# The meta tokens' share of an attention product, taken over 128 rows instead of 16, and one transpose moved to another PSUM buffer

## The chip, the cores and the metric

The kernel runs on one core of a Trainium2 chip. Its engines are TensorE (PE; its weight loads are shown apart as PEld), VectorE (DVE), ScalarE (ACT), GpSimd (POOL) and SyncE (SP), each with its own instruction queue and in step only through semaphores. The metric is the device time of one execution in microseconds (us); the lower the better. The median of three runs of the kernel before is 1240.04 us (1238.72 to 1245.06).

## The reference

One layer of a hybrid decoder, for one prompt of 512 tokens behind 16 learned meta tokens, and for 8 sequences that decode one token each over 2048 cached positions. RMSNorm, one input projection (2048 to 8192 columns), then eight heads of a gated linear recurrence and eight heads of differential attention, one output projection with the residual, final RMSNorm. All in float32. The part around the change is the attention of the prompt:

```python
def diff_attend(q, k, v, q_pos, k_pos, rel_bias, lam):
    s = jnp.einsum('bqhcd,bkhcd->bchqk', qf, kf) * (AT_DQK ** -0.5)
    dist = q_pos[:, None] - k_pos[None, :]
    bias = jnp.transpose(rel_bias[rel_bucket(dist)].astype(jnp.float32), (2, 0, 1))
    s = jnp.where(dist >= 0, s + bias, NEG_INF)
    p = jax.nn.softmax(s, axis=-1)
    w = p[:, 0] - lam * p[:, 1]
    return jnp.einsum('bhqk,bkhv->bqhv', w, v.astype(jnp.float32))
...
k_prompt (DEPTH, BATCH, N_META+SEQ, ...)   v_prompt   k_sample   v_sample    # new rows, also outputs
```

Keys 0 to 15 are the meta tokens, keys 16 to 527 the prompt. So the weights w of a block of 128 queries are a strip of 16 meta columns and one to four blocks of 128 columns, and the output is a sum of products over those blocks, the last of them over only 16 keys.

## The kernel before

**Projections.** The weights come in 128-column blocks (64 of the input projection, 16 of the output projection). ACT splits a group of four 128x128 tiles into a rounded part `hi` and DVE makes the rest `lo`; PE multiplies them with the split activations, 24 matmuls a group into the tile `ps`, four groups a block. The order is aq, ak, av (eight blocks each), then the recurrence's blocks, the gates, the output. One group is one slot of the main loop (line 1338); `split` runs three groups ahead (`LEAD`, line 296).

**Threads.** Everything else is written as Python generators that give out a few instructions in each slot, behind the group's matmuls: `attn_head`, `attn`, `hgrn`, the softmax of the decode sequences, and so on. `fill` and `value_step` add steps of the decode attention (key pages on DVE: `pgt`, `scd`; value pages on PE: `t_pv`) when a cost model of the five engines (class `Clock`) says that there is time and that a page has landed. Tiles taken through `tp` and `sc` are known to that model as rings of two PSUM buffers. All this happens while the program is written; on the chip each engine runs its list in that order.

**Attention of a head.** `to_tok` (lines 876 to 889) transposes the head's values on PE into two PSUM tiles of the ring `tp`: 24 rows (16 meta tokens and 8 samples) and 4 x 128 prompt rows. ACT copies both into one SBUF tile `vtok` of five 128-column parts (two buffers, shared with `ktok`), and three stores send the parts to the outputs from ACT's queue. `attn` (line 931) then works in steps n, four for a head; the block j of step n is scored at n, exponentiated at n+1, combined at n+2, transposed at n+3 and multiplied with the values at n+4. For two blocks together the output is built in the one PSUM buffer `o` (pool `psv`, tag `pv`) by matmuls of 256 columns (256 and 128 for the diagonal), and a last one, line 947, adds the meta tokens from 16 rows:

```python
T.matmul(o[:, :2 * P], a["vtok"][0:NM, 4, :], a["wmT"], start=False, stop=True)
```

Each float32 matmul is two in the trace. The transposes of a block, `t_w`, go to a `tp` buffer; the transposed meta strip fits beside them for blocks 0 to 2, and takes a second `tp` buffer, `t_w2`, for the fourth block (line 961). ACT copies them to `wT` and `wmT`.

When a head's block 3 is multiplied with the values, the step also holds the transposes of the values of the next head but one. Since the values of two heads fit in `vtok`'s buffers, ACT's copies there wait for the product `o` of the older head, which stands behind the transposes on PE; the next `t_w` takes the PSUM buffer of the 24 rows.

Of the kernel before, what the change touches and what calls it, by code (L numbers as in the profile page):

```python
# [18 lines left out]
P = 128  # L19
# [3 lines left out]
NS = 8  # L23
# [186 lines left out]
def layer_kernel(ctx: ExitStack, tc: tile.TileContext, A):  # L210
# [297 lines left out]
    lb = cp.tile([P, H], F32, name="lb")  # L508
    lb1 = cp.tile([P, H], F32, name="lb1")
    bm = cp.tile([P, 3, H], F32, name="bm")  # L510
    bdec = cp.tile([P, NPG, 2 * H], F32, name="bdec")
    b_far, b_near, b_new = bm[:, 0, :], bm[:, 1, :], bm[:, 2, :]
    rowd = dr.tile([H, W], F32, name="rowd")
    skew = dr.tile([H, P * W], F32, name="skew")
# [5 lines left out]
    def small_constants():  # L520
        t = tp("t_rows")
        T.transpose(t[:, :18], rows, ident[:18, :18])
        V.tensor_copy(cols, t[:, :18])
        V.tensor_scalar(gat, cols[:, 17:18], 1.0 - LAM_INIT, None, op0=ALU.mult)
        V.tensor_tensor(dp, dlv[:, :, 0, :], dlv[:, :, 1, :], op=ALU.mult)
        dsum = sm.tile([P, 2], F32, name="dsum", bufs=1)
        V.tensor_reduce(dsum, dp, axis=AX.X, op=ALU.add)
        lbm = sm.tile([P, H], F32, name="lbm", bufs=1)
        lbe = sm.tile([P, 2, H], F32, name="lbe", bufs=1)
        lbr = cols[:, 0:16].rearrange("p (r h) -> p r h", r=2)  # L530
        V.tensor_tensor(lbm, lbr[:, 0, :], lbr[:, 1, :], op=ALU.max)
        V.tensor_tensor(lbe, lbr, lbm.unsqueeze(1).to_broadcast([P, 2, H]), op=ALU.subtract)
        yield
        S.activation(dsum, dsum, AF.Exp)
        S.activation(lbe, lbe, AF.Exp)

        brow = hw.tile([H, W], F32, name="brow", tag="brow")
        for c0, c1 in ((0, 512), (512, W)):
            t = tp("t_br")
            T.matmul(t[:H, :c1 - c0], relb, oh[:, c0:c1], start=True, stop=True)  # L540
            V.tensor_scalar(brow[:, c0:c1], t[:H, :c1 - c0], -1.0, None, op0=ALU.mult)
        yield
        V.tensor_tensor(nlam, dsum[:, 1:2], dsum[:, 0:1], op=ALU.subtract)
        V.tensor_scalar(nlam, nlam, -LAM_INIT, None, op0=ALU.add)
        V.tensor_tensor(lbm, lbe[:, 0, :], lbe[:, 1, :], op=ALU.add)
        V.reciprocal(lbm, lbm)
        V.tensor_tensor(lb, lbe[:, 0, :], lbm, op=ALU.mult)
        V.tensor_scalar(lb1, lb, -1.0, 1.0, op0=ALU.mult, op1=ALU.add)
        yield
        store(out=rowd, in_=brow)  # L550
        t = tp("t_bm")
        for i in range(3):
            T.matmul(t[:, i * H:(i + 1) * H], oh[:, OF + i * P:OF + (i + 1) * P], relb, start=True, stop=True)
        V.tensor_copy(bm.rearrange("p m h -> p (m h)"), t[:, :3 * H])
        for c in range(2):
            bv = bdec.rearrange("p g (h c) -> p g h c", c=2)[:, :, :, c]
            V.tensor_copy(bv[:, 0:NPG - 1, :], b_far.unsqueeze(1).to_broadcast([P, NPG - 1, H]))
            V.tensor_copy(bv[:, NPG - 1, :], b_near)
        for h in range(H):
            yield  # L560
            store(out=skew[h].rearrange("(p w) -> p w", w=W), in_=rowd[h:h + 1, :].to_broadcast([P, W]))
        flag("const")
# [16 lines left out]
    gSa = cp.tile([P, H, NS], F32, name="gSa")  # L579
    amask = [cp.tile([P, P], F32, name=f"am{i}") for i in range(2)]  # L580
    ktail = [cp.tile([P, 2 * NM], F32, name=f"kt{i}") for i in range(2)]
    for a in amask + ktail:
        G.memset(a, 0.0)


# [211 lines left out]
    def softmax_dec(s):  # L797
        sco = scs[s]
        scp = sco[:, 0:NPG, :]
        V.tensor_tensor(scp, scp, bdec, op=ALU.add)  # L800
        V.tensor_copy(sco[:, NPG, :], snew[:, s].rearrange("p h c -> p (h c)"))
        mx = sm.tile([P, 2 * H], F32, name="mx", bufs=1)
        V.tensor_reduce(mx, sco.rearrange("p g a -> p a g"), axis=AX.X, op=ALU.max)
# [72 lines left out]
    def to_tok(src, h, name, tag, dst, dst_s):  # L876

        t2 = tp("t2_" + name)
        T.transpose(t2[:NM + NS, 0:P], src[:, NKEY:CT], ident)
        t = tp("t_" + name)  # L880
        for j in range(4):
            T.transpose(t[:, j * P:(j + 1) * P], src[:, NM + j * P:NM + (j + 1) * P], ident)
        tok = hw.tile([P, 5, P], F32, name=name, tag=tag, bufs=2)
        S.copy(tok[:NM + NS, 4, :], t2[:NM + NS, 0:P])
        S.copy(tok[:, 0:4, :].rearrange("p j d -> p (j d)"), t)
        store(out=dst[0, 0, NM:NKEY, h, :].rearrange("(j p) d -> p j d", p=P), in_=tok[:, 0:4, :])
        store(out=dst[0, 0, 0:NM, h, :], in_=tok[0:NM, 4, :])
        store(out=dst_s[0, :, 0, h, :], in_=tok[NM:NM + NS, 4, :])
        return tok

    def k_out(h):
        to_tok(ak[h], h, "ktok", "t5", A["k_prompt"], A["k_sample"])
# [20 lines left out]
    def attn_head(h):  # L913
        av = avs[h]
        strip = hw.tile([P, 528], F32, name="strip", tag="t1", bufs=2)
        flat = skew[h]
        clock.arrive(strip, 0.25)
        load(out=strip, in_=bass.AP(tensor=flat.tensor, offset=flat.offset, ap=[[W - 1, P], [1, 528]]))
        vtok = to_tok(av, h, "vtok", "t5", A["v_prompt"], A["v_sample"])
        G.tensor_copy(avS[:, :, h], av[:, T0:CT])  # L920
        for c in range(2):
            cs = slice(c * 64, (c + 1) * 64)
            G.tensor_copy(ktail[h % 2][cs, c * NM:(c + 1) * NM], ak[h][cs, SEQ:NKEY])
        heads[h] = dict(h=h, strip=strip, vtok=vtok, nm=sm.tile([P, 3, 4], F32, name="nm"),
                        s1=sm.tile([P, 4, 2], F32, name="s1"))
        flag(f"head{h}")
        yield
# [3 lines left out]
    def attn():  # L931
        live = {}
        for n in range(4 * H + 4):
            h, j = divmod(n, 4)
            if n < 4 * H and j == 0:
                if f"head{h}" not in flags or flags[f"head{h}"] >= slot[0]:
                    yield f"head{h}"
                head = heads[h]
            i4, i3, i2, i1 = (live.get(n - d) for d in (4, 3, 2, 1))
            if i4:  # L940
                a, jj = i4["head"], i4["j"]
                if jj % 2:
# [1 line left out]
                    for i in range(jj):  # L944
                        T.matmul(o[:, :2 * P], a["vtok"][:, i, :], a["wT"][:, (2 * i + 1) * P:(2 * i + 3) * P], start=i == 0, stop=False)
                    T.matmul(o[:, P:2 * P], a["vtok"][:, jj, :], a["wT"][:, 0:P], start=False, stop=False)
                    T.matmul(o[:, :2 * P], a["vtok"][0:NM, 4, :], a["wmT"], start=False, stop=True)
                    S.copy(aq[:, a["h"], (jj - 1) * P:(jj + 1) * P], o[:, :2 * P])
                if jj == 3:
                    flag(f"attn{a['h']}")  # L950
# [2 lines left out]
            if i3:  # L953
# [4 lines left out]
                for i in range(jj + 1):  # L958
                    x = NM + (i - odd) % (jj + 1) * P
                    T.transpose(t[:, i * P:(i + 1) * P], i3["p"][0][:, x:x + P], ident)  # L960
                t2, c2 = (t, L2) if jj < 3 else (tp("t_w2"), 0)
                T.transpose(t2[:NM, c2:c2 + P], i3["p"][0][:, 0:NM], ident)
                if not odd:
                    a["wT"] = hw.tile([P, 7 * P], F32, name="wT", tag="t4", bufs=1)
                    a["wmT"] = sm.tile([NM, 2 * P], F32, name="wmT", tag="wmT", bufs=1)
                w2 = a["wT"].rearrange("p (c q) -> p c q", q=P)
                S.copy(w2[:, 0:2 * jj + 1:2] if odd else w2[:, 1:2 * jj + 2:2], t[:, :L2].rearrange("p (c q) -> p c q", q=P))
                S.copy(a["wmT"][:, odd * P:(odd + 1) * P], t2[:NM, c2:c2 + P])
            if i1:
                a, L1 = i1["head"], (i1["j"] + 1) * P + NM  # L970
                for c in range(2):
# [47 lines left out]
    def hgrn(h):  # L1019
# [23 lines left out]
        vt = tp("t_hvt")  # L1043
        for j in range(4):
            T.transpose(vt[:, j * P:(j + 1) * P], v[:, NM + j * P:NM + (j + 1) * P], ident)
        hv8 = sm.tile([NS, P], F32, name="hv8", tag="wmT", bufs=1)
        S.copy(hv8, t[:NS, 0:P])
        store(out=hvd[h], in_=hv8)
        vkm = sm.tile([NM, 2, P], F32, name="vkm", bufs=1)
# [376 lines left out]
```

## Time and profile before

| | |
|---|---|
| median of three runs (lowest to highest) | 1240.04 us (1238.72 to 1245.06) |
| the profiled execution | 1245.11 us |
| its span, first to last instruction | 1243.3 us |
| PE busy / DVE / ACT / POOL | 97% / 72% / 43% / 12% |
| mean granted clock of TensorE | 0.990 of full speed |
| PE's share of the chain that ended last | 79% (`ps` alone 65%) |

The attention of the prompt lies between about 258 and 470 us of the span, with its value products from 267 us on. A row of the timeline gives start, duration, engine, line, operation, the tile written and those read, the count, and in brackets the idle time of the engine before it with what ended it. All compute instructions have line 168, the helper that records them, so the tiles' names tell them apart. A PE that the profile calls busy may still stream less than it could: the weight load before a matmul and the time between two starts show that.

### The profile page before, as it was taken

How to read it: one execution, taken by the hardware profiler on the slowest of the kernel's cores; microseconds unless marked ns; L12 is line 12 of the kernel's file. 1: busy time of each engine (PE TensorE's matmuls, PEld its weight loads, DVE VectorE, ACT ScalarE, POOL GpSimd, SP SyncE). 2: the span in 40 equal slices, each digit the busy share in tenths (PEclk: the TensorE clock that was granted, in tenths of full speed). 3: DMA queues.
4: the chain of work that ended last, by engine and by line, in shares of the span. 5: the costliest groups of instructions: out<-in, count | busy, mean ns of one | idle time of the engine just before them, and what ended most of it. 6: DMA issues, size and time to landing. Idle time of an engine off the chain costs nothing.

```text
span 1243.3 us, 24937 instructions
## 1 busy us (share of the span) xinstructions
PE 1207.9 (97%) x9352; PEld 1094.5 (88%) x9352; DVE 897.7 (72%) x1678; ACT 532.6 (43%) x1255; POOL 143.2 (12%) x151
## 2 busy tenths in 40 slices
PE   8999999999999999999999999999999999999995
PEld 6899999986677677888888889999999999999995
DVE  7522498878888888878897886989988956345253
ACT  6322333344545564445355465565422235323223
POOL 2000000100000000012010120122123310022020
PEclk9999999999999999999999999999999999999998
DMA  7353788836666669888888976757978837432223
GB/s 232 98 161 93 238 280 289 287 119 220 223 224 207 187 215 305 287 279 267 290 276 289 324 242 204 240 169 243 268 215 247 257 99 238 115 91 86 86 69 138
DMA packets 240958, 261.03 MB, mean 210 GB/s; under 512 B 8783, under 2 KB 198962, under 8 KB 240171
## 3 DMA queue, kind: packets, MB, share of 16 engines
q1 hardware_dynamic: 57298, 164.09, 38.3%
q10 hardware_dynamic: 183538, 95.34, 27.0%
q8 instruction: 74, 1.21, 0.4%
q14 instruction: 48, 0.39, 0.1%
HBM read 245.94 MB, written 16.14 MB: 211 GB/s over the span
## 4 chain that ended last, share of the span: by engine, by line
PE 79%; DVE 10%; DMA 4%; ACT 3%; issue 2%; ACTq 1%; SPq 0%; DVEq 0%
PE ps L168 65%; PE t_pv L168 4%; DVE qb L168 2%; DVE pgt L168 2%; DVE scd L168 2%; PE o L168 1%; PE ho L168 1%; DVE lo L168 1%; DMA raw<-in_w_out 1%; PE sc L168 1%; DMA raw<-in_w_in 1%; PE up L168 1%; PE t_w L168 1%; PE at L168 1%; DVE p L168 1%
## 5 line engine op out<-in xcount | busy, mean ns | idle before, releaser
L168 PE MATMUL ps<-xh,hi 128*128 128x264 f32 (+2 forms) x2048 | 539.8, 294 | 1.2 <-ACT ak L168 0.8
L168 PE MATMUL ps<-xl,hi 128*128 128x264 f32 (+2 forms) x2048 | 522.5, 286 | 1.1 <-DVE xl L168 1.1
L168 PEld LDWEIGHTS ps<-xh,hi 128*128 128x128 f32 x2048 | 387.5, 189 | 51.6 <-issue 41.7
L168 DVE TENSOR_TENSOR lo<-raw,hi 128x512 fp32r<-128x512 f32 x321 | 253.5, 795 | 216.5 <-ACT hi L168 215.6
L168 PEld LDWEIGHTS ps<-xl,hi 128*128 128x128 f32 x2048 | 388.0, 189 | 2.8 <-issue 2.7
L168 PE MATMUL ps<-xh,lo 128*128 128x264 f32 (+2 forms) x2048 | 333.1, 285 | 0.0
L168 ACT CAST hi<-raw 128x512 fp32r<-128x512 f32 x321 | 196.2, 617 | 242.9 <-PE ps L168 196.0
L168 PEld LDWEIGHTS ps<-xh,lo 128*128 128x128 f32 x2048 | 283.9, 189 | 0.0
L168 DVE TENSOR_TENSOR pgt<-pgt,qb 128x1024 f32<-128x1024 f32 x128 | 156.3, 1221 | 11.7 <-DMA pgt<-in_cache_k 7.0
L168 DVE TENSOR_REDUCE scd<-pgt 128x16 f32<-128x1024 f32 x128 | 155.6, 1216 | 1.7
L168 PE MATMUL ps<-mh,hi 128*128 128x256 f32 (+1 forms) x512 | 129.9, 286 | 0.2 <-ACT y L168 0.2
L168 PE MATMUL ps<-ml,hi 128*128 128x256 f32 (+1 forms) x512 | 128.5, 283 | 0.0
L168 DVE SCALAR_TENSOR_TENSOR qb<-pgt,wd,qb 128x128 f32<-128x128 f32 x360 | 106.8, 371 | 0.0
L168 PEld LDWEIGHTS ps<-mh,hi 128*128 128x128 f32 x512 | 96.5, 188 | 0.7 <-ACT y L168 0.4
L168 PEld LDWEIGHTS ps<-ml,hi 128*128 128x128 f32 x512 | 96.6, 189 | 0.0
L168 PE MATMUL ps<-mh,lo 128*128 128x256 f32 (+1 forms) x512 | 82.4, 283 | 0.0
L168 PEld LDWEIGHTS ps<-mh,lo 128*128 128x128 f32 x512 | 70.3, 189 | 0.0
L168 PE MATMUL t_pv<-pgt,wd 128*32 128x512 f32 x320 | 48.2, 648 | 8.5 <-ACT wmT L168 4.6
L168 POOL TENSOR_TENSOR sd<-sd,vb 128x1024 f32<-128x1024 f32 x8 | 19.4, 2430 | 174.5 <-ACT vb L168 174.5
L168 ACT COPY hgm<-ho 128x128 f32<-128x128 f32 x32 | 8.5, 265 | 70.0 <-PE ho L168 69.9
L168 ACT ACTIVATE p<-p,nm 128x144 f32<-128x144 f32 (+3 forms) x64 | 36.1, 565 | 2.0 <-DVE nm L168 2.0
L168 DVE TENSOR_TENSOR xr<-xr,t_y 128x512 f32<-128x512 f32 (+1 forms) x17 | 11.2, 657 | 31.2 <-PE t_y L168 31.2
(242 smaller groups left out, 1156.0 us busy)
## 6 DMA issues: line engine op xcount, KB each, us to landing
pgt<-in_cache_k SPq DMA_DIRECT2D x128, 512.0 KB
pgt<-in_cache_v SPq DMA_DIRECT2D x128, 512.0 KB
raw<-in_w_in ACTq DMA_DIRECT2D x125, 512.0 KB
raw<-in_w_out ACTq DMA_DIRECT2D x32, 512.0 KB
x<-in_x_prompt SPq DMA_DIRECT2D x4, 1024.0 KB
qb<-qd SPq DMA_DIRECT2D x8, 512.0 KB
sd<-in_state_hgrn SPq DMA_DIRECT2D x8, 512.0 KB
vb<-hvd SPq DMA_DIRECT2D x8, 512.0 KB
```

What stands on the lines that cost most here:

```text
L168: r = f(*a, **k)
```

## The change

1. The meta rows of the values get a tile of their own, `few` (24 x 128, one buffer), in place of the fifth part of `vtok`; `hv8` of the recurrence shares its tag. `vtok` has four parts.
2. Two constant tiles `vmeta` (128 x 128) and one `wmeta` (128 x 256) are zeroed once by POOL. Once a head ACT copies the 16 meta rows of `few` into `vmeta`; the transposed meta weights go to the first 16 rows of `wmeta` instead of `wmT`. The last matmul of `o` runs over all 128 rows, of which 112 are zeros.
3. The fourth block's `t_w2` comes from `psv`, the buffer of `o`, instead of the ring `tp`, and is no longer known to the cost model.
4. The bias of the decode scores, `bdec`, holds its two different rows instead of sixteen; adding it takes two DVE instructions instead of one.

```diff
@@ small_constants
-    bdec = cp.tile([P, NPG, 2 * H], F32, name="bdec")
+    bdec = cp.tile([P, 2, 2 * H], F32, name="bdec")
...
-            bv = bdec.rearrange("p g (h c) -> p g h c", c=2)[:, :, :, c]
-            V.tensor_copy(bv[:, 0:NPG - 1, :], b_far.unsqueeze(1).to_broadcast([P, NPG - 1, H]))
-            V.tensor_copy(bv[:, NPG - 1, :], b_near)
+            V.tensor_copy(bdec.rearrange("p g (h c) -> p g h c", c=2)[:, :, :, c], bm[:, 0:2, :])
...
-    for a in amask + ktail:
+    vmeta = [cp.tile([P, P], F32, name=f"vm{i}") for i in range(2)]
+    wmeta = cp.tile([P, 2 * P], F32, name="wmeta")
+    for a in amask + ktail + vmeta + [wmeta]:
         G.memset(a, 0.0)
@@ softmax_dec
-        V.tensor_tensor(scp, scp, bdec, op=ALU.add)
+        V.tensor_tensor(sco[:, 0:NPG - 1, :], sco[:, 0:NPG - 1, :], bdec[:, 0, :].unsqueeze(1).to_broadcast([P, NPG - 1, 2 * H]), op=ALU.add)
+        V.tensor_tensor(sco[:, NPG - 1, :], sco[:, NPG - 1, :], bdec[:, 1, :], op=ALU.add)
@@ to_tok
-        tok = hw.tile([P, 5, P], F32, name=name, tag=tag, bufs=2)
-        S.copy(tok[:NM + NS, 4, :], t2[:NM + NS, 0:P])
-        S.copy(tok[:, 0:4, :].rearrange("p j d -> p (j d)"), t)
-        store(out=dst[0, 0, NM:NKEY, h, :].rearrange("(j p) d -> p j d", p=P), in_=tok[:, 0:4, :])
-        store(out=dst[0, 0, 0:NM, h, :], in_=tok[0:NM, 4, :])
-        store(out=dst_s[0, :, 0, h, :], in_=tok[NM:NM + NS, 4, :])
-        return tok
+        tok = hw.tile([P, 4, P], F32, name=name, tag=tag, bufs=2)
+        few = sm.tile([NM + NS, P], F32, name="few", tag="few", bufs=1)
+        S.copy(few, t2[:NM + NS, 0:P])
+        S.copy(tok.rearrange("p j d -> p (j d)"), t)
+        store(out=dst[0, 0, NM:NKEY, h, :].rearrange("(j p) d -> p j d", p=P), in_=tok)
+        store(out=dst[0, 0, 0:NM, h, :], in_=few[0:NM, :])
+        store(out=dst_s[0, :, 0, h, :], in_=few[NM:NM + NS, :])
+        return tok, few
@@ attn
                 head = heads[h]
+                S.copy(vmeta[h % 2][0:NM, :], head["few"][0:NM, :])
...
-                    T.matmul(o[:, :2 * P], a["vtok"][0:NM, 4, :], a["wmT"], start=False, stop=True)
+                    T.matmul(o[:, :2 * P], vmeta[a["h"] % 2], wmeta, start=False, stop=True)
...
-                t2, c2 = (t, L2) if jj < 3 else (tp("t_w2"), 0)
+                t2, c2 = (t, L2) if jj < 3 else (psv.tile([P, 512], F32, name="t_w2", tag="pv"), 0)
...
-                    a["wmT"] = sm.tile([NM, 2 * P], F32, name="wmT", tag="wmT", bufs=1)
...
-                S.copy(a["wmT"][:, odd * P:(odd + 1) * P], t2[:NM, c2:c2 + P])
+                S.copy(wmeta[0:NM, odd * P:(odd + 1) * P], t2[:NM, c2:c2 + P])
@@ hgrn
-        hv8 = sm.tile([NS, P], F32, name="hv8", tag="wmT", bufs=1)
+        hv8 = sm.tile([NS, P], F32, name="few", tag="few", bufs=1)
```

Three places show what the change does to the instruction lists. The first is ACT's list at the step with a head's last product, before (`vtok` are the values, `aq<-o` is the copy of the product, `raw` a load of projection weights):

```order
L168 COPY vtok<-t_vtok 24x128 [waits PE_49]
L168 COPY vtok<-t_vtok 128x512
L886 DMA out_v_prompt<-vtok 128x4x128 [waits DMAHW3_49,Activation_49]
L887 DMA out_v_prompt<-vtok 16x128 [waits DMAHW4_49]
L888 DMA out_v_sample<-vtok 8x128 [waits DMAHW6_49]
L168 COPY aq<-o 128x256
L168 COPY wT<-t_w 128x128 [waits PE_49]
```

The same place now, with the first instructions of the next step:

```order
L168 COPY few<-t_vtok 24x128 [waits DMAHW3_49,DMAHW2_49,PE_49]
L168 COPY vtok<-t_vtok 128x512 [waits PE_49]
L888 DMA out_v_prompt<-vtok 128x4x128 [waits Activation_49]
L889 DMA out_v_prompt<-few 16x128 [waits DMAHW4_49]
L890 DMA out_v_sample<-few 8x128 [waits DMAHW5_49]
L168 COPY aq<-o 128x256 [waits PE_49]
L168 COPY wT<-t_w 128x128 [waits PE_49]
L168 COPY wmeta<-t_w 16x128
L168 ACTIVATE p_3602,s_3385<-p_3602,nm 128x400 [waits DVE_49]
L168 ACTIVATE p_3604,s_3385<-p_3604,nm 128x400 [waits DVE_49]
L168 CAST hi<-raw 128x512
L168 COPY vm_504<-few 16x128
```

The order is kept but for the new copy `vm` at the next step's head. What each copy waits for has changed: before, one wait on PE stood at the 24 rows and covered both copies and `aq<-o`; now the 24 rows wait for their own transpose and for two earlier stores (the DMAHW names), and the 512 columns and `aq<-o` each for PE.

The second place is PE's list at the fourth block's transposes of the seventh head, before (`sc` are scores, `t_sum` belongs to the softmax of a decode sequence):

```order
L168 MATMUL t_w<-ident,p_5581 128x128 [waits DVE_49,Activation_49]
L168 MATMUL t_w<-ident,p_5581 128x128 x3
L168 MATMUL t_w_5813<-ident,p_5581 16x128 [waits DVE_49]
L168 MATMUL sc<-ak_2916,aq 128x400 x2
L168 MATMUL t_sum<-rs,ones 128x16 [waits Activation_49]
```

and now:

```order
L168 MATMUL t_w<-ident,p_5598 128x128 [waits DVE_49,Activation_49]
L168 MATMUL t_w<-ident,p_5598 128x128 x3
L168 MATMUL t_w_5830<-ident,p_5598 16x128
L168 MATMUL sc<-ak_2927,aq 128x400 [waits DVE_49] x2
L168 MATMUL t_sum<-rs,ones 128x16 [waits DVE_49]
```

Nothing moves here, but the matmul behind the transposes no longer waits for ACT's copy of `t_w`, since it takes the other buffer of the ring.

The third place is PE's list in the recurrence of the first head, as a piece of the difference (`up` are state updates, `t_mx` is of a decode softmax):

```order
 L168 MATMUL up<-hvtok,hktok 128x128 x2
 L168 MATMUL t_mx<-ident,mx 16x128
-L168 MATMUL t_pv<-pgt,wd 32x512 x4
 L168 MATMUL ps<-xh_111,hi 128x272
 L168 MATMUL ps<-xl_115,hi 128x272
@@ -2260,4 +2259,5 @@
 L168 MATMUL at<-qe,hf 128x128
 L168 MATMUL up<-hvtok,hktok 128x128 x2
+L168 MATMUL t_pv<-pgt,wd 32x512 x4
```

A value step goes one slot later, because the cost model's times have shifted. The same happens to some ten value steps and to the ends of three decode sequences; DVE's page steps and a few page loads move with them. The counts are the same, and from about the middle of PE's list and the last quarter of DVE's on they are in the old order again.

## Rows read from the trace of the kernel before

**Rows 1.** The page, part 1: busy time, share of the span, instructions.
```profile
PE 1207.9 (97%) x9352; PEld 1094.5 (88%) x9352; DVE 897.7 (72%) x1678; ACT 532.6 (43%) x1255; POOL 143.2 (12%) x151
```
**Rows 2.** Windows by stage: stretch, length, busy time by engine, PEclk, DMA share, GB/s.
```profile
260.00:290.00 30.00, 28.64 (x191) 21.86 (x191) 27.23 (x71) 13.19 (x42) 1.79 (x4) 0.94 0.60 184
...
700.00:1000.00 300.00, 297.66 (x2408) 282.50 (x2407) 262.26 (x595) 135.48 (x311) 62.40 (x41) 1.00 0.75 235
```
**Rows 3.** The timeline of PE, three steps of the attention.
```profile
279.29 1.68 PE L168 MATMUL o<-wT,vtok 128*128 128x256 f32 x8
280.90 0.69 PE L168 MATMUL o<-wmT,vtok 16*128 16x256 f32 x2
281.94 0.44 PE L168 MATMUL t_w<-ident,p 128*128 128x128 f32 x2 [0.34 <-ACT vtok L168]
...
294.03 0.81 PE L168 MATMUL o<-wT,vtok 128*128 128x256 f32 x4
294.78 0.69 PE L168 MATMUL o<-wmT,vtok 16*128 16x256 f32 x2
295.40 0.66 PE L168 MATMUL t_w<-ident,p 128*128 128x128 f32 x4
```
**Rows 4.** The timeline of ACT at the first of those steps, and later.
```profile
281.63 0.73 ACT L168 COPY vtok<-t_vtok 24x128 f32<-24x128 f32 x2 [6.02 <-PE o L168]
...
283.83 0.37 ACT L168 COPY aq<-o 128x256 f32<-128x256 f32 x1 [1.47 <-issue]
...
290.60 0.37 ACT L168 COPY wT<-t_w 128x256 f32<-128x256 f32 x1 [4.35 <-PE t_w L168]
```
**Rows 5.** Groups by line and shape: count, busy us and mean ns, idle before.
```profile
L168 ACT COPY wmT<-t_w 16x128 f32<-16x128 f32 x32 | 8.0, 249 | 0.0
...
L168 ACT COPY vtok<-t_vtok 128x512 f32<-128x512 f32 x8 | 4.6, 575 | 0.4 <-PE t_vtok L168 0.4
...
L168 DVE TENSOR_TENSOR scd<-scd,bdec 128x256 f32<-128x256 f32 x8 | 3.3, 417 | 0.0
```
**Rows 6.** Who waited for whom: us in total, times, longest us.
```profile
PE t_pv L168 <- ACT wmT L168: 4.6, 6, 0.9
PE t_pv L168 <- DVE st L168: 2.4, 3, 1.2
PE t_w L168 <- ACT vtok L168: 2.1, 6, 0.3
PE t_sum L168 <- ACT wT L168: 1.1, 1, 1.1
...
ACT hi L168 <- DMA out_k_prompt<-ktok: 6.3, 1, 6.3
```
**Rows 7.** Windows of 3.4 us behind three of the waits, columns as before.
```profile
284.32:287.72 3.40, 3.16 (x13) 1.50 (x14) 3.26 (x12) 1.93 (x7) 0.00 (x0) 0.50 1.02 312
...
420.85:424.25 3.40, 3.40 (x15) 1.74 (x16) 2.34 (x9) 1.96 (x6) 0.00 (x0) 0.50 0.98 255
311.62:315.02 3.40, 2.66 (x21) 1.74 (x21) 3.01 (x10) 2.74 (x9) 0.00 (x0) 1.00 0.83 243
```
**Rows 8.** The chain that ended last, in order of time: start, us, what.
```profile
55.62 72.53 PE ps L168 x600
...
284.56 1.94 PE t_pv L168 x8
286.50 3.74 PE ps L168 x24
...
312.44 1.07 PE t_pv L168 x8
313.51 3.16 PE ps L168 x24
...
420.80 1.93 PE t_pv L168 x8
422.73 3.87 PE ps L168 x24
```

More of the change, by code (lines that the diff above doesn't have):

```diff
@@ L918, in attn_head @@
         load(out=strip, in_=bass.AP(tensor=flat.tensor, offset=flat.offset, ap=[[W - 1, P], [1, 528]]))
-        vtok = to_tok(av, h, "vtok", "t5", A["v_prompt"], A["v_sample"])
+        vtok, few = to_tok(av, h, "vtok", "t5", A["v_prompt"], A["v_sample"])
         G.tensor_copy(avS[:, :, h], av[:, T0:CT])
@@ L923, in attn_head @@
             G.tensor_copy(ktail[h % 2][cs, c * NM:(c + 1) * NM], ak[h][cs, SEQ:NKEY])
-        heads[h] = dict(h=h, strip=strip, vtok=vtok, nm=sm.tile([P, 3, 4], F32, name="nm"),
+        heads[h] = dict(h=h, strip=strip, vtok=vtok, few=few, nm=sm.tile([P, 3, 4], F32, name="nm"),
                         s1=sm.tile([P, 4, 2], F32, name="s1"))
```

## The prediction

> **What bounds the kernel now.** The page's busy times come first: PE is busy for 97% of the span, the next engine for 72% [rows 1]. Then the windows by stage: from 700 us to 1000 us PE is busy 297.66 of 300 us, but from 260 to 290 us, in the attention, 28.64 of 30, and there the granted clock is 0.94, which no busy time shows [rows 2]. So PE sets the end nearly everywhere, and what PE gains in the attention should come off the end, if no other engine takes over. In that window DVE is busy 27.23 of 30 us [rows 2]; it is the candidate.
>
> Inside the attention the timeline of PE shows what is slow [rows 3]. A step that ends a pair of query blocks runs its `o` matmuls over 128 rows, then two over 16 rows. The list of waits has PE idle before `t_pv` for ACT's copy `wmT` (4.6 us in 6 steps), before `t_w` for ACT's copy `vtok` (2.1 us, 6 steps) and once before `t_sum` for `wT` (1.1 us) [rows 6]. Last, the windows of 3.4 us right behind these waits: in four of the six steps the granted clock is 0.50, the lower level of 1.2 GHz (the first and the last of the four stand in [rows 7]), in the other two 1.00 (one is shown).
>
> **The 16-row product.** Eight matmuls of `o` (six of 256 columns, two of 128) take from 279.29 to the next start at 280.90, 1.61 us; four (two of 256, two of 128) from 294.03 to 294.78, 0.75 us [rows 3]. The difference, four of 256 columns, is 0.86, so 0.215 us each. That leaves 0.32 for the two of 128 columns and what follows; two at half of 0.215 are 0.215, so about 0.10 us passes at the change from 128 rows to 16. The two 16-row matmuls then take from 294.78 to 295.40, 0.62 us, where two of 128 rows would take 0.43. Over 128 rows each group should be 0.10 + 0.19 = 0.29 us shorter. There are 16 groups, two for each of 8 heads. In the eight groups of the first pair PE waits for nothing behind them: 8 x 0.29 = 2.3 us. Of the eight of the second pair, two stand in steps without new values (the last two heads): the full 0.29 for one, 0.2 for the other, where `t_pv` follows at once and still has its own change of shape before it: 0.5 us. The other six are in the next part. As bounds I take nothing (the time between the starts stays) and 16 x 0.29 = 4.6.
>
> The Trainium skill speaks against this term: "TensorE: Matmul & The Clock Gate" (LDWEIGHTS, in Part 2, and the table under "Why this matters for your kernels") says that a weight load's time depends on its columns and not on its rows, and that a matmul with 32 rows takes as long as one with 128. By that rule the 2.8 us fall away, and the sum below would be 1233.4 instead of 1230.6. The starts in the timeline of PE contradict it at this place, 0.31 us against 0.215 for the same 256 columns [rows 3], so I go by them.
>
> **The wait of the value copies.** In six steps ACT's copy of the 24 rows stands idle for 6.02 us until the product `o` is done and starts at 281.63, 0.04 us after the 16-row matmuls end (280.90 + 0.69) [rows 3, 4]. The two copies end at 282.36; for 1.47 us ACT's queue issues three stores; the copy `aq<-o` starts at 283.83 [rows 4]; then come `wT` and `wmT`, and `t_pv` starts at 284.56 [rows 8]. Now the 24 rows have a tile of their own and are copied early, and the 512 columns of `vtok` wait only for the last matmul that reads `vtok`, at 279.29 + 1.68 = 280.97. With the same 0.04 the copy starts at 281.01, takes 0.575 [rows 5] and ends at 281.59, 0.77 us earlier, and with it the stores, `aq`, `wT`, `wmeta` and `t_pv`. PE can follow: the second of the two products starts `t_w` at about 281.23 instead of 281.94 [rows 3], since the buffer of the 24 rows is free by then. What is late next is the same chain: about 0.7 us of waiting before `t_pv` stays, with the three stores in it. Gain 6 x 0.77 = 4.6 us; bounds 6 x 0.29 = 1.7 (only the product is shorter) and 6 x (0.77 + 0.35) = 6.7, were the old `t_w` wait to go besides.
>
> **The buffer of `t_w2`.** The fourth block's strip leaves the ring, so the next user of the ring takes a buffer that has long been read. The one case where PE stood for it is `t_sum`, 1.1 us [rows 6]; I take 1.1, bounds 0 and 1.1. In `psv` the strip follows an `o` that was copied a step earlier, and the next `o` needs its copy anyway.
>
> **The clock.** From the start of `t_pv` to the end of the 24 matmuls behind it a step at full clock takes 1.07 + 3.16 = 4.23 us; the first half-clock step takes 1.94 + 3.74 = 5.68, the last 1.93 + 3.87 = 5.80 [rows 8]. Each dip costs 1.45 to 1.57, four about 6.0 us. Each begins in the wait before `t_pv`, after 16-row matmuls, transposes, 64-row scores and idle time. From the end of the full-row products to `t_pv` that is 284.56 - 280.90 = 3.7 us; it becomes 283.79 - 281.23 = 2.6 us, and the product before it works with 128 rows. Two of the six steps waited alike and had no dip (`t_pv` at 312.44 in [rows 8], clock 1.00 in [rows 7]), so the length alone doesn't decide. I take all four dips as gone: bounds 0 and 6.0.
>
> **Edits costed at nothing.** Eight copies `vm` are like `wmT` at 0.25 us [rows 5], on ACT at a point where it idles 4.35 us [rows 4]; without that cover 2 us. Eight more additions on DVE cost at most as much as the one they split, 0.42 us [rows 5], 3.3 us together, in DVE's idle time (2.8 of 30 us in [rows 2] where it is fullest). Two fewer copies of `bdec` and three more memsets fall in or near a stretch in which PE runs 72.53 us of projections without a wait [rows 8]. The value steps that go a slot later keep their matmuls; their waits on `st` are 2.4 us now [rows 6] and may go or double: 0, bounds -2.4 and +2.4.
>
> **The sum.** Against the profiled execution: 1245.11 - 2.3 - 0.5 - 4.6 - 1.1 - 6.0 = 1230.6 us. It is the slow end of the three runs, 5.1 us over their median of 1240.04. Four dips at 1.5 us nearly span the 6.3 us between lowest and highest, so the median run probably had one dip or none (an inference, its trace isn't here); from it the sum would be 1240.04 - 8.5 - 1.5 = 1230.0 with one and 1231.5 with none.
>
> **Rivals.**
> 1. The dips stay. For it: transposes, 64-row scores and about 0.7 us of idle time remain before `t_pv`. Against it: the stretch is 30% shorter, and already now it doesn't always dip. Time: 1230.6 + 6.0 = 1236.6. A rule of the Trainium skill points this way: "TensorE: Matmul & The Clock Gate", Part 4, says that transposes don't count as PE work for the clock; by it the step still offers little. That a dip can be absent after the same transposes is in the windows [rows 7].
> 2. The chain on ACT doesn't start earlier, because the `vtok` copy or the stores find another wait (the stores of the head before). For it: ACT has stood 6.3 us for such a store [rows 6]. Against: one time, in the stage of the keys. Then 4.6 becomes 1.7: 1233.5, and 1239.5 if the dips stay too.
> 3. DVE takes over in the attention. It is busy 27.23 of 30 us [rows 2]; with 8.5 + 6.0 us taken from some 200 it would have to fit the same work in 93% of the time, 0.91 of it now. Against: most windows are below that one. If a third of the 14.5 us is lost, 1235.4.
> 4. Slower: `few` has one buffer, so the copy of the 24 rows, at the front of ACT's queue with the `hi` casts behind it, waits for two stores of the head before. If those land later than the next head's copy, ACT stands in each of the seven later key heads. At the one wait of its kind, 6.3 us [rows 6], that is 44 us; the lead of three groups (3 x 3.16 = 9.5, from [rows 8]) covers it once: +34.6 us, 1265. It decides from about 2.5 us a head on (7 x 2.5 = 17.5 = 9.5 + 8). Against: `ktok`'s two buffers showed one wait in eight heads.
>
> **How the numbers follow.** What a measurement of this kernel can tell from no change is about 0.5%, 6.2 us: below 1233.8 is faster, above 1246.2 slower. Forecast 0.68, all of it below 1233.8. Dips stay 0.12 (1233.8 to 1237, no change). ACT's chain 0.09 (around 1233.5 to 1239.5; a third of it counts as faster). DVE 0.06 (no change). Slower 0.05. So faster 0.68 + 0.03 = 0.71, same 0.24, slower 0.05. The range starts at the forecast less the remaining bounds (the old `t_w` wait 2.1, `st` 2.4, in part): 1227; it reaches to 1237.5, over rival 1 and most of 2 and 3.
>
> **What would show it.** Right: `o` from `wmeta` at 0.215 us between starts and `t_w` straight behind it; no wait of `t_w` for `vtok`; ACT's copy `few` early and `vtok` just after the last `o` from `wT`; `t_pv` still waiting about 0.7 us in six steps; `t_sum` without its wait; a granted clock of 1.00 from 260 to 470 us; the stage that ended at 470 us ends about 14.5 us earlier. Wrong: a start to start of 0.3 us for the new product, dips in the same steps, `few` in ACT's list of waits for stores, or a stage that is shorter by 14 us while the span is not, which would put the bound on DVE behind it.

## The result and the profile after

The changed kernel takes 1226.95 us (median of six runs, 1224.27 to 1229.12), the kernel before beside it 1239.18 (six runs, 1238.07 to 1245.06). The ratio is 0.989, with a 95% interval of 0.988 to 0.991. Timed again, it was 1225.53 beside 1240.86, ratio 0.987 (0.984 to 0.991). That is faster by more than the 0.5% that can be told, as forecast, and in the attention by the mechanism that was forecast. But 1226.95 is 3.65 us below the predicted 1230.6 and 0.05 us below the low end of the range. Where those 3.65 us come from is the main question of the experiments. One run of a later kernel (rows_apart, 1309.44 us at a mean clock of 0.85) was disturbed and counts in no median or fit below.

The profiled execution of the changed kernel took 1229.12 us, the slowest of its six; the one of before took 1245.11. The page's first part:

```profile
span 1227.3 us, 24956 instructions
## 1 busy us (share of the span) xinstructions
PE 1197.7 (98%) x9352; PEld 1093.3 (89%) x9352; DVE 897.4 (73%) x1684; ACT 534.4 (44%) x1263; POOL 142.2 (12%) x154
```

Against [rows 1] PE has lost 10.2 us of busy time with the same number of instructions, and DVE is as busy as it was: the gain is on PE. The windows that answer to [rows 2]:

```profile
260.00:290.00 30.00, 28.84 (x210) 23.22 (x209) 26.77 (x70) 14.99 (x49) 0.71 (x4) 1.00 0.61 185
700.00:1000.00 300.00, 298.18 (x2413) 283.73 (x2412) 257.64 (x604) 132.32 (x298) 63.49 (x43) 1.00 0.72 226
```

The granted clock in the attention is 1.00 (0.94 before), and DVE is no busier there than it was (26.77 of 30 us, 27.23 before). PE's timeline in the step that answers to the first rows of [rows 3], and in the step with the four matmuls of the first pair:

```profile
279.57 1.68 PE L168 MATMUL o<-wT,vtok 128*128 128x256 f32 x8
281.09 0.60 PE L168 MATMUL o<-wmeta,vm 128*128 128x256 f32 x2
281.53 0.38 PE L168 MATMUL t_w<-ident,p 128*128 128x128 f32 x2
...
284.12 1.06 PE L168 MATMUL t_pv<-pgt,wd 128*32 128x512 f32 x8 [0.81 <-ACT wmeta L168]
...
292.14 0.81 PE L168 MATMUL o<-wT,vtok 128*128 128x256 f32 x4
292.79 0.60 PE L168 MATMUL o<-wmeta,vm 128*128 128x256 f32 x2
293.22 0.60 PE L168 MATMUL t_w<-ident,p 128*128 128x128 f32 x4
```

From start to start the four take 0.65 us (0.75 in [rows 3]) and the two over 128 rows 0.43 (0.62 over 16). `t_w` starts right behind them. Where the rows cost time shows in the weight loads (PEld). Two rows of before, then the two that answer to them:

```profile
294.77 0.29 PEld L168 LDWEIGHTS o<-wmT,vtok 16*128 16x128 f32 x2
295.40 0.37 PEld L168 LDWEIGHTS t_w<-ident,p 128*128 128x128 f32 x4 [0.33 <-issue]
...
292.68 0.30 PEld L168 LDWEIGHTS o<-wmeta,vm 128*128 128x128 f32 x2
293.01 0.52 PEld L168 LDWEIGHTS t_w<-ident,p 128*128 128x128 f32 x4
```

Before, the first load of the 16 rows and the first load behind them begin together with their matmuls (294.77 and 294.78 us, 295.40 both). Now they begin 0.11 and 0.21 us ahead of them (292.68 and 292.79, 293.01 and 293.22). Whether these missing leads are the whole 0.29 us of a group is not shown.

`t_pv` still waits, 0.81 us here. ACT's timeline at the same place, to be read against [rows 4] (ACTq is the issue of a store from ACT's queue):

```profile
278.77 0.25 ACT L168 COPY few<-t_vtok 24x128 f32<-24x128 f32 x1 [2.99 <-PE t_vtok L168]
281.29 0.58 ACT L168 COPY vtok<-t_vtok 128x512 f32<-128x512 f32 x1 [2.27 <-PE o L168]
281.91 0.39 ACTq L888 DMA_DIRECT2D out_v_prompt<-vtok  x1
...
283.39 0.37 ACT L168 COPY aq<-o 128x256 f32<-128x256 f32 x1 [1.51 <-PE se L168]
```

The 24 rows are copied as soon as they are transposed; `vtok` starts 0.04 us after the last `o` from `wT` ends (279.57 + 1.68). The 1.51 us ahead of `aq` are put down to PE by the view, but they are the three stores that stand between the two rows. PE's waits, against [rows 6]:

```profile
PE t_pv L168 <- ACT wmeta L168: 4.9, 6, 1.0
...
PE ho L168 <- DVE am L168: 1.2, 1, 1.2
...
PE t_pv L168 <- DVE st L168: 0.6, 1, 0.6
```

The waits of `t_w` for `vtok` and of `t_sum` for `wT` are gone, the wait of `t_pv` in six steps stays about as long as it was (4.9 us, 4.6 before), and of the three waits for `st` one is left.

By stages, from the first projection block of the attention to the first block behind it: 226.09 to 481.94 before (255.85 us), 226.58 to 467.88 now (241.30). That is 14.55 us less; the forecast for this profiled execution had 14.5. Ahead of it 0.5 us were lost; behind it, to the end, 1.9 us more were gained, and that sum hides a gain and a loss. The first nine projection blocks behind the attention are 4.3 us shorter (157.3 before, 153.0 now, with one value step of 1.1 us that now stands behind them), the rest is 2.4 us longer. PE's timeline of before, the `t_pv` and the softmax steps between 490 and 523 us:

```profile
490.22 0.28 PE L168 MATMUL t_mx<-ident,mx 128*16 128x128 f32 x1
491.74 1.06 PE L168 MATMUL t_pv<-pgt,wd 128*32 128x512 f32 x8 [1.25 <-DVE st L168]
501.69 0.39 PE L168 MATMUL t_mb<-ident,m 16*128 16x16 f32 x2
502.64 1.06 PE L168 MATMUL t_pv<-pgt,wd 128*32 128x512 f32 x8 [0.56 <-DVE st L168]
511.36 1.07 PE L168 MATMUL t_pv<-pgt,wd 128*32 128x512 f32 x8
519.25 0.29 PE L168 MATMUL t_sum<-rs,ones 128*128 128x16 f32 x2
520.06 2.25 PE L168 MATMUL t_pv<-pgt,wd 128*32 128x512 f32 x8 [0.53 <-ACT hf L168]
```

and now:

```profile
476.15 0.28 PE L168 MATMUL t_mx<-ident,mx 128*16 128x128 f32 x1
480.64 1.07 PE L168 MATMUL t_pv<-pgt,wd 128*32 128x512 f32 x8
486.10 0.39 PE L168 MATMUL t_mb<-ident,m 16*128 16x16 f32 x2
490.65 1.90 PE L168 MATMUL t_pv<-pgt,wd 128*32 128x512 f32 x8
499.70 1.07 PE L168 MATMUL t_pv<-pgt,wd 128*32 128x512 f32 x8
503.75 0.29 PE L168 MATMUL t_sum<-rs,ones 128*128 128x16 f32 x2
```

Before, each of the three softmax steps had a `t_pv` at its heels, and each of these waited. Now none has. For the first two the code says why: in a slot of the recurrence the second `up` takes one buffer of the ring `tp`, the softmax step the other, and a `t_pv` behind both has to wait until DVE's `st` has read the first. This is the third place in the section on the change. The third `t_pv`, at 520 us, is another case: no `up` stands in its slot, its wait is put down to ACT, and its second half waited for a value page to land, as its weight loads show:

```profile
521.26 0.14 PEld L168 LDWEIGHTS t_pv<-pgt,wd 128*32 128x32 f32 x4 [1.05 <-DMA pgt<-in_cache_v]
```

The `t_pv` of 1.90 us at 490 us now is long for the same reason. More moves than the "some ten value steps" of the section on the change: by the traces 23 of the 40 value steps stand one to three slots later. The loss (1.2 us of `ho` for `am`, and smaller ones) varies: the second profile of the same kernel, with a span of 1224.1, doesn't have that wait, and is 2.7 us shorter than the first one behind these nine blocks (from 620 us on).

### The profile page after: what moved, and what is told of

Same layout as the page of the kernel before. It is cut to its first block, busy times and chain, and to the rows that moved or that the text cites. A ratio compares the mean times of both kernels' runs of the same rounds, so it can differ in the third digit from the quotient of the medians.

```text
span 1227.3 us, 24956 instructions
## 1 busy us (share of the span) xinstructions
PE 1197.7 (98%) x9352; PEld 1093.3 (89%) x9352; DVE 897.4 (73%) x1684; ACT 534.4 (44%) x1263; POOL 142.2 (12%) x154
## 4 chain that ended last, share of the span: by engine, by line
PE 85%; DVE 6%; DMA 5%; ACT 3%; issue 1%; ACTq 1%; SPq 0%; DVEq 0%
PE ps L168 69%; PE t_pv L168 3%; DMA raw<-in_w_in 2%; PE o L168 1%; DVE qb L168 1%; PE ho L168 1%; PE sc L168 1%; DMA raw<-in_w_out 1%; DMA qb<-qd 1%; DVE scd L168 1%; PE t_w L168 1%; PE up L168 1%; DVE pgt L168 1%; DVE lo L168 1%; PE t_y L168 1%
```

## The experiments

Theory A says that some 3 us came from the later value steps in the recurrence, beside the forecast terms; theory B that all of it is in the attention. Times differ by the half-clock stretches that a run happens to have (3.4 us at a granted clock of 0.50, the prediction's dips), so beside the medians there is a fitted time: one straight line over the runs of the kernels below and the 60 of before beside them, a level for each kernel and one common slope, which comes out at 1.33 us for 0.001 of a run's mean granted clock. The level is read at 0.996, the clock of a run without such a stretch in the attention or the recurrence. Its standard errors are about 0.5 to 0.7 us, for before 0.3; a difference from before has 0.5 to 0.7, a difference from the changed kernel about 0.95. With the first six runs of the changed kernel taken in as well, its level is 1226.3 in place of 1225.8.

| kernel | median, us | median of before beside it | fitted |
|---|---|---|---|
| before | 1241.0 (60 runs) | | 1238.2 |
| after_again | 1225.53 | 1240.86 | 1225.8 |
| plan_old | 1229.88 | 1240.86 | 1228.6 |
| ring_only | 1227.46 | 1240.86 | 1227.3 |
| psv_alone | 1235.86 | 1240.86 | 1233.8 |
| narrow | 1229.77 | 1240.38 | 1229.5 |
| rows_apart | 1239.82 | 1240.38 | 1237.2 |
| late_store | 1221.67 | 1240.38 | 1222.8 |
| guard_before | 1242.97 | 1240.38 | 1238.7 |
| rows_apart_bdec | 1234.22 | 1241.42 | 1232.8 |
| guard_some | 1236.42 | 1241.42 | 1235.3 |
| late_before | 1235.45 | 1241.42 | 1233.3 |
| late_again | 1222.05 | 1241.42 | 1222.7 |

### The order of the value steps and the buffer of t_w2

after_again has no edit.

> The changed kernel once more, with a second profile. Theory A (some 3.7 us of the gain come from the value steps that run a slot later in the recurrence): 1226 to 1228 us, and the stage from the end of the attention to the last value step is again 2 to 6 us shorter than before, where the list of waits shows fewer waits of t_pv. Theory B (the whole gain is in the attention, and the first trace of the changed kernel was a chance one): the recurrence comes out within 1 us of before, and the attention is some 15 us shorter in the trace although the kernel before has no half-clock stretches in most of its runs.

1225.53 us. The waits for `st` are again 0.6 us, once; between the attention's end and 583 us (the 35th block) it takes 115.6 us (467.48 to 583.09), before took 120.3 (481.94 to 602.26).

plan_old:

```diff
-t2, c2 = (t, L2) if jj < 3 else (psv.tile([P, 512], F32, name="t_w2", tag="pv"), 0)
+t2, c2 = (t, L2) if jj < 3 else (clock.tile(psv.tile([P, 512], F32, name="t_w2", tag="pv"), "tp", 2), 0)
```

> The changed kernel, but the model that places the value steps still believes that t_w2 takes a buffer of the ring tp, so that all 23 value steps stand where they stood before; t_w2 itself is in the output's buffer. Theory A (the later value steps are worth about 3.7 us): 1230.5 us, 3 to 4 us above the changed kernel. Theory B (all the gain is in the attention): 1227 us, as the changed kernel.

1229.88 us; fitted, it is 2.8 us above the changed kernel (2.3 with its first six runs taken in). PE's waits of plan_old:

```profile
PE t_pv L168 <- DVE st L168: 2.6, 3, 1.4
```

They are back as in [rows 6], and the trace differs from the second one of the changed kernel at this place: from the keys to the attention's end the two run in step to 0.5 us; one block later plan_old has lost 3.9 us, of which 1.0 is a value step that it does earlier, and at the recurrence's end 1.8 us of it are left. The first trace of the changed kernel, with its wait of `ho`, has lost 2.6 us against the second by then, so one trace against another decides little there. The first nine blocks behind the attention decide more: 155.6 to 161.0 us in the five profiles with the old order (the longest has a half-clock stretch in it, some 1.5 us), 152.1 to 153.4 in the eight with the new one (guard_before, below, has an order of its own). The one value step carried beyond them is 1.1 us of the difference. Theory A, at the lower end of its price.

ring_only:

```diff
-t2, c2 = (t, L2) if jj < 3 else (psv.tile([P, 512], F32, name="t_w2", tag="pv"), 0)
+t2, c2 = (t, L2) if jj < 3 else (pst.tile([P, 512], F32, name="t_w2", tag="tp"), 0)
```

> The changed kernel, with the order of every engine the same, but t_w2 really takes a buffer of the ring tp. The forecast has 1.1 us for that buffer (one wait of t_sum for wT): 1228 us, with that wait back or another one of about that length. Theory C (the buffer, not the order, is what shortens the recurrence's neighbours): 1230 us or more. Were the buffer worth nothing: 1227.

1227.46 us, 1.4 us above (fitted), which is not clear of its error by itself; the expected wait is there:

```profile
PE t_sum L168 <- ACT wT L168: 1.1, 1, 1.1
```

psv_alone (the kernel before):

```diff
-t2, c2 = (t, L2) if jj < 3 else (tp("t_w2"), 0)
+t2, c2 = (t, L2) if jj < 3 else (psv.tile([P, 512], F32, name="t_w2", tag="pv"), 0)
```

> The kernel before with t_w2 in the output's buffer and nothing else: the 16-row product, the copies and bdec stay; the value steps move as in the changed kernel. Theory A: 1239.2 - 1.1 - 3.7 = 1234.4 us. Theory B: 1238.1 (the one wait of t_sum alone). If half-clock stretches cost time in its runs, they show in its trace from 260 to 470 us as before.

1235.86 us, 4.4 us below before (fitted), 5.0 in the medians: about the sum of order (2.8) and buffer (1.4) from the other side. The half-clock stretches stayed, two in its trace.

guard_before and guard_some leave `t_w2` where it was and move the value steps by a rule of their own (`used` counts the uses of `tp` in a slot):

```diff
@@ value_step
+        if landed and "attn7" in flags and used.get(slot[0], 0) >= 2:          # guard_before
+        if landed and n < 27 and "attn7" in flags and used.get(slot[0], 0) >= 2:   # guard_some
+            return
```

> The kernel before with one rule more in the plan of the value steps: behind the last head of the attention a slot in which the ring tp was already used twice or more gets no value step. t_w2 keeps its buffer of the ring. The steps 18 to 27 of the 43 stand then where the changed kernel has them, the later ones one to five groups later still. Theory A (what the later value steps gain is the wait of t_pv for a buffer that DVE's st has to read first, in slots in which up and a strip of the softmax took the ring's two buffers): the waits t_pv for st (2.4 us in 3 steps) and the long step at 520 us go, 3 to 4 us less than before. Rival (it is not the ring but chance in the order of pages and transfers): within 1.5 us of before.

A miss: 1242.97 us, as slow as before, or slower. The waits for `st` are gone, but new ones came:

```profile
PE ho L168 <- DVE am L168: 4.5, 2, 2.4
...
PE t_mx L168 <- DVE mx L168: 1.6, 1, 1.6
```

All three are waits for DVE, behind 800 us. Why DVE is late there was not followed up: the value steps from the 28th on stand up to six slots later than in the changed kernel, and what DVE does between them moves with them. With these steps moved as well the rule was no test of the theory, so it was cut down:

> The kernel before with the rule of guard_before, for the value steps up to number 27 alone: every value step then stands where the changed kernel has it, and nothing else is changed; t_w2 keeps the ring. Theory A (the order of the value steps is worth 2.8 us by itself, since a slot with up and a strip of the softmax leaves no free buffer of the ring): 2.8 us less than before, 1237.6 where before is at 1240.4, with the waits of t_pv for st down from 2.4 to about 0.6 us. Rival (in plan_old and psv_alone it was something else than the order): as before.

1236.42 us, 2.8 us below before (fitted, standard error 0.5), 5.0 in the medians, with every value step where the changed kernel has it and nothing else changed:

```profile
PE t_pv L168 <- DVE st L168: 0.6, 1, 0.6
```

So the order alone gives the 2.8 us, shown from both kernels. The waits for `st` are 1.8 of it.

### The 128-row product and the copies

narrow (the changed kernel):

```diff
-T.matmul(o[:, :2 * P], vmeta[a["h"] % 2], wmeta, start=False, stop=True)
+T.matmul(o[:, :2 * P], vmeta[a["h"] % 2][0:NM, :], wmeta[0:NM, :], start=False, stop=True)
```

> The changed kernel, with the meta product over 16 rows again: it reads the upper 16 rows of vm and wmeta, all else and the order of every engine stay. Theory A (rows cost time at this place, as the starts in the timeline say): o from wmeta takes about 0.31 us from start to start instead of 0.22, and 0.1 us passes at the change from 128 rows to 16. In the six steps with new values ACT's chain of copies, which no longer hangs on this product, sets the end and hides it; ten groups x 0.29 to 0.34 = 2.9 to 3.4 us remain: about 1229.5 us, from 1226 to 1227 for the changed kernel. Rival (a matmul of 16 rows takes as long as one of 128): 1226.5 us, and the same starts as with 128 rows. If the 16 rows make the clock fall, half-clock stretches come back in the attention and it is above 1231.

1229.77 us, 3.7 above the changed kernel (fitted). Its timeline and its waits:

```profile
278.78 0.82 PE L168 MATMUL o<-wT,vtok 128*128 128x256 f32 x4
279.53 0.69 PE L168 MATMUL o<-wmeta,vm 16*128 16x256 f32 x2
280.15 0.44 PE L168 MATMUL t_w<-ident,p 128*128 128x128 f32 x2
```
```profile
PE t_pv L168 <- ACT wmeta L168: 2.8, 6, 0.7
```

The starts are those of before again (0.75 and 0.62 us), and the weight loads begin together with their matmuls again. In the steps with new values the time goes into the wait, which falls to 2.8 us (4.9 and 4.6 in the two profiles of the changed kernel); the other ten groups are about 0.32 us longer each, 3.2 us in the traces of the attention. A half-clock stretch did not come back.

rows_apart (the kernel before):

```diff
-        tok = hw.tile([P, 5, P], F32, name=name, tag=tag, bufs=2)
+        tok = hw.tile([P, 4, P], F32, name=name, tag=tag, bufs=2)
+        few = sm.tile([NM + NS, P], F32, name="few", tag="few", bufs=2)
...
-T.matmul(o[:, :2 * P], a["vtok"][0:NM, 4, :], a["wmT"], start=False, stop=True)
+T.matmul(o[:, :2 * P], a["few"][0:NM, :], a["wmT"], start=False, stop=True)
```

> The kernel before, in which only the 24 short rows of keys and values get a tile of their own (few, two buffers), read by the 16-row product as it is; t_w2, wmT, bdec and the value steps stay as before. Theory A (the chain of copies on ACT is what PE waits for): the value copy starts when the last o from wT ends, 0.6 to 0.8 us earlier in six steps, 3.6 to 4.8 us less than before: 1235.5 us where before is at 1240; the wait of t_w for vtok goes. Rival (the copy starts earlier, but the stores or aq keep the end of the chain): 1239 to 1240. The half-clock stretches: if the 16 rows cause them they stay in its trace; if the length of the wait does, they go, and 2 to 3 us more with them.

1239.82 us: nothing gained, and it proves neither side, since the edit did not do what it was meant to:

```profile
PE t_w L168 <- ACT few L168: 2.1, 6, 0.3
```

The wait has only changed its name: `few` with two buffers is read by the product of two heads before, just as `vtok` is. One half-clock stretch stands in its attention. With a third buffer (`bufs=3`, and the two-row `bdec` of the change to make room):

> As rows_apart, with a third buffer for few (room for it comes from the two-row bdec, which is in this kernel too). In rows_apart the copy of the 24 rows still stood for the product, since few with two buffers was read by the product of two heads before; with three it does not. Theory A (the chain of copies on ACT is what PE waits for): the wait of t_w is gone, the value copy starts when the last o from wT ends, 4.2 us less in six steps: 1236 us where before is at 1240.4, less if half-clock stretches go too. Rival (the stores or aq keep the end of the chain, or the split of bdec's addition costs DVE as much): 1239 to 1240.

1234.22 us, 5.4 us below before (fitted), 7.2 in the medians. No wait of `t_w`, and of the wait of `t_pv` half is left:

```profile
PE t_pv L168 <- ACT wmT L168: 2.4, 6, 0.5
```

2.1 + (4.6 - 2.4) = 4.3 us of waits have gone, so the release of the value copy, with no 128-row product, is worth about what the forecast had for it (4.6). The two-row `bdec` is in this kernel too; no wait of PE names it.

### The remaining wait, and the clock

late_store (the changed kernel), late_again (the same once more) and late_before (the kernel before) issue the three stores of the values a slot later:

```diff
-    def to_tok(src, h, name, tag, dst, dst_s):
+    def to_tok(src, h, name, tag, dst, dst_s, send=store):
...
-        store(out=dst[0, 0, NM:NKEY, h, :].rearrange("(j p) d -> p j d", p=P), in_=tok)
+        send(out=dst[0, 0, NM:NKEY, h, :].rearrange("(j p) d -> p j d", p=P), in_=tok)
...
-        vtok, few = to_tok(av, h, "vtok", "t5", A["v_prompt"], A["v_sample"])
+        vtok, few = to_tok(av, h, "vtok", "t5", A["v_prompt"], A["v_sample"], lambda **k: later(1, **k))
```

> The changed kernel, with the three stores of the values issued a slot later, behind ACT's copies aq, wT and wmeta instead of ahead of them; no value step moves. Theory A (the three stores, 1.47 us on ACT, hold up the remaining wait of t_pv for wmeta, 4.6 to 4.9 us in six steps): the wait goes, 1221.5 us. Rival (the copies themselves or PE's t_w are just as late): less than 1.5 us, 1225 to 1226.

> The changed kernel with the later stores once more, with another profile: 1221 to 1222 us, 4 us below the changed kernel; no wait of t_pv for wmeta. If the half-clock stretch at 747 us of the first profile belongs to this kernel and not to that one run, it is there again.

1221.67 and 1222.05 us, ratios to before 0.985 and 0.984 (0.981 to 0.989, 0.981 to 0.988): the fastest version here, 3.5 to 3.9 us below the changed kernel in the medians, 3.0 to 3.1 fitted. Two of late_store's five runs took 1227 to 1228 us; one of them is its profiled one. PE's timeline of late_again in the step shown above:

```profile
281.93 0.41 PE L168 MATMUL se<-kt,aq 128*128 128x32 f32 x2
282.27 1.06 PE L168 MATMUL t_pv<-pgt,wd 128*32 128x512 f32 x8
```

`t_pv` follows at once. The half-clock stretch in late_store's profile, at 747 us, was not there in the second.

> The kernel before with the three stores of the values a slot later and nothing else: 16-row product, t_w's wait and the value copies stay as they are. The wait of t_pv for wmT (4.6 us in six steps) should go. Theory A (the half-clock stretches begin in that wait): they go with it, some 2 to 3 us more in the median: 1233 us where before is at 1240.4. Rival (they come from the 16-row product and the transposes around it, or from t_w's wait): the granted clock still falls behind some of the six steps, and it is 1236.

1235.45 us, 4.9 us below before (fitted). The wait for `wmT` is 0.2 us, and its trace has no half-clock stretch in the attention; but its runs' mean clocks, 0.993 to 0.997, say that some runs still have one or two somewhere. Between the two theories that is undecided.

## Why the prediction was right in the attention and short in the size

**The attention: right.** 14.55 us of 14.5 in the profiled pair. The product over 128 rows takes 0.43 us and the change of shape is gone, 1.08 us for the group instead of 1.37 (the forecast 0.29). Worked out for ten groups at 0.29 the term was 2.8; the pair has 3.2, and so has narrow's trace. By the Trainium skill, "TensorE: Matmul & The Clock Gate" (LDWEIGHTS, in Part 2, and the table under "Why this matters for your kernels"), the rows would have given nothing. The traces agree with it on the load alone, 0.18 us over 16 rows and 0.19 over 128; on the time between starts narrow disagrees, by 3.2 us in its trace and 3.7 fitted. In the steps with new values, from the start of `o` to `t_pv`, 5.27 us became 4.55 in the step shown, and the six became 0.70 shorter on average, of the 0.77 forecast. The remaining wait was put at 0.7 a step; it is 0.8.

**The buffer of t_w2: right.** 1.1 forecast; the wait of 1.1 us comes back with the ring (ring_only), and 1.4 us fitted, with an error of 0.95.

**The step that failed** is this term: "The value steps that go a slot later keep their matmuls; their waits on `st` are 2.4 us now [rows 6] and may go or double: 0, bounds -2.4 and +2.4." It is -2.8 us (guard_some), beyond its bound. In the profiled pair the two waits for `st` (1.25 + 0.56) are the ring's, and they go. The rest was in neither bound: at 520 us a wait of 0.53 and the 1.18 that its `t_pv` took beyond 1.07 go, and now one at 490 us takes 0.83 beyond it. Together that is 2.7. Such long steps are a matter of the run as well: in the first 45 us behind the attention, what `t_pv` takes beyond 1.07 us comes to 0.5 to 2.2 us in the five profiles with the old order (with the 0.53 counted in) and to 0 to 1.0 in the eight with the new. The sign could have been read: the rows of the third place in the section on the change show `t_pv` leaving the slot of `up` and `t_mx`, and the ring has two buffers. The range took this bound and another "in part"; taken whole it would have started at 1230.6 - 2.1 - 2.4 = 1226.1 and held the result.

The sum was made for the profiled execution, and 1.5 of the 3.65 us lie between it and the changed kernel's own profiled execution (1229.12); the other 2.2 lie between that run, which has the loss behind 620 us, and the median of its six. Without half-clock stretches the forecast's terms make 8.5 us; fitted, the kernels are 12.3 apart (standard error 0.7; 11.8 with the first six runs taken in). The order's 2.8 is most of the 3.8 between; the rest, 1.0, is within the errors of the fit.

**The clock: right in the pair, wrong for the median.** All four half-clock stretches of the attention are gone. They were put at 6.0 us, 1.5 each; guard_some's attention, which is the code of before and has one where before's profile has four, is 4.5 us shorter. "Each begins in the wait before `t_pv`" is not quite what the trace shows: two of the four begin 0.05 and 0.2 us behind it. And "the median run probably had one dip or none" was too low: the runs of before have a median of the mean clock of 0.994, and other profiles at 0.994 have one or two such stretches; at 1.33 us for 0.001 the 0.002 up to 0.996 are 2.7 us, which is between one and two.

**The rivals.** The dips did not stay; ACT's copies did start earlier; DVE did not take over (26.77 of 30 us). `few` with one buffer cost one wait of 0.3 us of `t_vtok`, not 2.5 us a head. The edits costed at nothing beside the value steps (the copies `vm`, the two additions of `bdec`) are named by no wait of PE.

## What to carry over

When a change moves an instruction out of a slot, count who uses the ring of buffers in that slot: with two buffers the third user waits for another engine (0.6 to 2.1 us here), and its going is worth the wait, not nothing. Release a copy by what reads the old contents, not only by giving it a tile: two buffers read by the same late reader wait as one. Stores issued from a compute engine's queue stand in front of its next copies (1.51 us for three); issuing them a slot later took 3 to 4 us off here.

## What the runs showed of the hardware

- Apart from the end of the span, the 14 profiles show 13 half-clock stretches, all 3.4 us long, in or up to 1.3 us behind a wait of PE of 0.7 to 2.4 us. One stands in the recurrence of late_store, where `ho` had waited for DVE:

```profile
746.69 0.46 PE L168 MATMUL ho<-am,hvtok 128*128 128x128 f32 x2 [1.84 <-DVE am L168]
```
```profile
747.30:750.70 3.40, 3.40 (x18) 2.95 (x17) 3.30 (x6) 1.95 (x6) 1.43 (x1) 0.50 0.54 176
```

- In the attention nine half-clock stretches fell on the 30 steps (five profiles) in which `t_w` waits 0.35 us and `t_pv` 0.7 to 0.9; none on the 54 steps of the other nine profiles, in which one of the two waits is missing or both are. Neither the 16 rows (narrow) nor one of the waits alone goes with a stretch there. That the two waits together cause it is likely, not shown: the same code has one stretch in one run and four in another, and other instructions differ between the two groups of kernels too.
- A weight load over 16 rows and the first one behind it begin together with their matmuls, in before and in narrow alike, where over 128 rows they begin 0.11 and 0.21 us ahead of them; the load itself is about as long (0.18 and 0.19 us).
